# A hybrid decoder trunk: linear attention's scores as five products, mixers' operands in halves of 64 columns, and attention's second value product over half the keys

## The chip, the core and the metric

The kernel runs on one core of one Trainium2 chip. Its engines work side by side, each through its own instructions in order: TensorE (PE; PEld is its loading of weights), VectorE (DVE), ScalarE (ACT), GpSimd (POOL) and SyncE (SP, which here only starts DMAs). PE writes to PSUM banks; DVE and ACT copy from there to SBUF. The metric is the device time of one execution in microseconds, lower is better.

## What is computed

Two layers, 1024 tokens, model width 1024, everything in f32. A layer projects the normalised input once, feeds three groups of heads (the "mixers"), gates their outputs and projects back. The three mixers, cut to what the change touches:

```python
def sliding_window_attention(q, k, v, sinks):          # 8 heads of 64, 2 kv heads, blocks of 128
    kk, vv = with_prev(kb), with_prev(vb)              # a block sees its own keys and the block before
    rel = i + ATTN_BLOCK - j
    valid = (rel >= 0) & (rel < WINDOW)                # 128 keys back, the own one included
    p = softmax(concatenate([where(valid, s, -1e30), sink]))[..., :-1]
    return einsum('bnhgqk,bnkhd->bnqhgd', p, vv)

def retention(q, k, v):                                # 4 heads of 64, chunks of 128
    def step(state, inp):
        sc = einsum('bhid,bhjd->bhij', qi, ki) * dmask
        intra = einsum('bhij,bhjv->bhiv', sc, vi)
        inter = einsum('bhid,bhdv->bhiv', qi * q_decay, state)
        return chunk_decay * state + einsum('bhjd,bhjv->bhdv', ki * k_decay, vi), intra + inter

def gated_linear_attention(q, k, v, log_a):            # 4 heads, key width 32, value width 64
    def step(state, inp):
        b = cumsum(gi, axis=2)                         # per key channel
        decay = where(causal, exp(minimum(b_i - b_j, 0.0)), 0.0)
        sc = einsum('bhid,bhijd,bhjd->bhij', qi, decay, ki)
        intra = einsum('bhij,bhjv->bhiv', sc, vi)
        inter = einsum('bhid,bhdv->bhiv', qi * exp(b), state)
        return exp(b_last) * state + einsum('bhjd,bhjv->bhdv', ki * exp(b_last - b), vi), intra + inter
```

## The kernel before

Tokens are tiled by 128: eight tiles t, four pairs p. A layer runs through the columns of the projection in units of 256 (`do_gqk`, `do_kv` and so on). The projections are products of f32r halves into the three PSUM banks called `mm`; all the rest on PE, the mixers' products and the transposes, goes to the five banks called `aux`, which are handed out in turn. Each mixer is a generator, a "job": `attn_two` (two tiles of one kv head g), `ret_two` (two tiles of retention), `gla_decays` and `gla_core` (two chunks of linear attention).

PE's order is written out while the program is recorded. A clock `clk` counts the cost that each product is said to have (`mult` adds it); a job that yields `lat(key, l)` is taken up again when `clk` has gone on by the number that the table `L` has under that key (with `@1` for the second layer), and meanwhile the projections are recorded. PE then runs what is recorded in that order and waits where an operand is late. The order on ACT, DVE, POOL and SP within a layer's body is the framework's scheduler's.

A product names an operand that is loaded as weights (`lhsT`, up to 128 rows and 128 columns) and one that streams past (`rhs`). Where operands start at other partitions than 0, or the weights have 64 or 32 columns, only a part of the array is used: a tile of so many rows and columns. In the profile "32*128" is such a shape of weights, rows by columns; a product of f32 operands shows up as two records (two passes), one of f32r as one.

The steps that the change touches, by the names that the profile has for them:

- linear attention's scores, in `gla_core`: for a chunk c and a head h (32 rows) three products of blocks (`kxz` by `q1`, 32 columns streaming) and four of the sub-blocks of 8 (`kds` by `ad`), 28 products for the four heads, each with 128 columns of weights ("aux<-t,mx" and "aux<-t" 32*128). Each head has its own `aux` bank, sp[h]. ACT (L1774) and DVE (L1775, under the mask `mask2`) copy them to `scz`.
- linear attention's value products: `qb` by the state `stG`, then `scz` by v ("aux<-t,mx" 128*128 128x64); then `pst`, the new state, in tiles of 32 columns ("aux<-t,t" 128*32).
- retention: scores of 64 rows by 128 columns ("aux<-t" 64*128), then the state product ("aux<-stR,t"), the values ("aux<-t,t" 128*128 128x64) and the new state `pst` ("aux<-t,t" 128*128 128x128).
- attention's value products in `attn_two`: the transposed softmax `pf` by the value tile of the block before ("aux<-t,va" 128*64), then the part of it that lies in the own block (`pr`, cut out on POOL at L1545) by the difference of the two value tiles, `vd` (made on POOL at L1497; "aux<-t,vd").
- the columns of the modulation in `mod_third` ("aux<-c_ones,acc").

Of the kernel before, what the change touches and what calls it, by code (L numbers as in the profile page):

```python
# [61 lines left out]
def host_constants():  # L62
# [9 lines left out]
    c["mask2"] = ((i[:, None] <= i[None, :]) & (i[:, None] // 32 == i[None, :] // 32)).astype(np.int32)  # L72
# [96 lines left out]
def trunk(ctx: ExitStack, tc: tile.TileContext, ins, cst, out):  # L169
# [242 lines left out]
    def mod_third(l, j):  # L412
# [17 lines left out]
        for hh in range(2):  # L430
# [1056 lines left out]
    def attn_two(l, ts, g, q):  # L1487

        sms, parts, pss = {}, {}, {}
        for t in ts:  # L1490
            sm = sms[t] = gp.tile([P, 4, 129], F32, tag="smx", name=nm("smx"), bufs=SMB)
            V.tensor_copy(sm[:, :, 128], sink8[:, l, 4 * g:4 * g + 4])
            if t == 0:
                G.memset(sm[:, :, 0:128], -1e30)
            else:
                vd = gp.tile([P, P], F32, tag="vd", name=nm("vd"), bufs=4)
                G.tensor_tensor(vd, kv["v"][t], kv["v"][t - 1], ALU.subtract)  # L1497
                parts[t] = vd
# [37 lines left out]
        for t in ts:  # L1536
# [5 lines left out]
            mv[t] = [(kv["v"][max(t - 1, 0)], pf)]  # L1542
            if t > 0:
                pr = t2()
                G.affine_select(h4(pr), h4(pf), [[0, 4], [1, P]], ALU.is_ge, 0.0, base=0, channel_multiplier=-1)  # L1545
                mv[t].append((parts[t], pr))
        yield lat("aq4", l)
        po = aux()
# [6 lines left out]
        copy("aoc", ao, po)  # L1555
# [117 lines left out]

    def cb32(ap):
        return ap.rearrange("p (c b i) -> p c b i", c=2, i=32)

    def gla_decays(l, p):
# [21 lines left out]
        midv = mid.rearrange("p (b s) -> p b s", s=4)  # L1699
        for s, dst in enumerate((dC[:, 0:64], dC[:, 64:192], dC[:, 192:384], dB[:, 256:512])):  # L1700
            n = 8 * s + 8
            eng(f"ak{s}").tensor_tensor(dst.rearrange("p (b i) -> p b i", i=n),
                                        midv[:, :, s:s + 1].to_broadcast((P, 8, n)), b32(bc)[:, :, 0:n], ALU.subtract)
# [15 lines left out]
    QSC = 32.0 ** -0.5  # L1719

    def gla_core(l, p, qk, vs):
# [7 lines left out]
        k = qk[:, 256:512]  # L1729
# [5 lines left out]
        for s, src in enumerate((dC[:, 0:64], dC[:, 64:192], dC[:, 192:384])):  # L1735
            n = 8 * s + 8
            eng(f"kd{s}").tensor_tensor(b32(kdz[:, s])[:, :, 0:n], b32(k)[:, :, 0:n],
                                        src.rearrange("p (b i) -> p b i", i=n), ALU.mult)
        kds = [kdz[:, 0], kdz[:, 1], kdz[:, 2], ad[:, 256:512]]
        for s in range(4, 0, -1):  # L1740
            kv_ = kxz[:, s - 1].rearrange("p c (b i) -> p c b i", i=32)
            eng(f"kx{s}").tensor_tensor(kv_[:, :, 0:s, :], cb32(k1)[:, :, 0:s, :],
                                        g[:, :, 4 * s:5 * s].unsqueeze(3).to_broadcast((P, 2, s, 32)), ALU.mult)
# [9 lines left out]
        for c in range(2):  # L1753
# [9 lines left out]
            yield lat("gcs", l)  # L1763
            for s in range(4):
                for h in range(4):
                    r = slice(32 * h, 32 * h + 32)
                    dst = sp[h][:, 0:P].rearrange("p (b i) -> p b i", i=32)[:, :, 8 * s:8 * s + 8]
# [705 lines left out]
```

## Time and profile before

| | us |
|---|---|
| median of 3 timed executions | 964.28 (964.02 to 966.57) |
| the profiled execution | 965.28 |
| its span, first to last instruction | 963.6 |
| PE busy in the span | 944.9 |
| DVE, ACT, POOL busy | 670.1, 392.7, 176.8 |
| mean granted clock of TensorE | 0.999 of full |

The profiled execution took 1.0 us more than the median of the others. The mixers' products on PE run from 108 to 430 us in the first layer and from 584 to 861 us in the second, between the projections' products; what lies ahead of and between the two prepares a layer or ends it, and the last output follows.

### The profile page before, as it was taken

How to read it: one execution, taken by the hardware profiler on the slowest of the kernel's cores; microseconds unless marked ns; L12 is line 12 of the kernel's file. 1: busy time of each engine (PE TensorE's matmuls, PEld its weight loads, DVE VectorE, ACT ScalarE, POOL GpSimd, SP SyncE). 2: the span in 40 equal slices, each digit the busy share in tenths (PEclk: the TensorE clock that was granted, in tenths of full speed). 3: DMA queues.
4: the chain of work that ended last, by engine and by line, in shares of the span. 5: the costliest groups of instructions: out<-in, count | busy, mean ns of one | idle time of the engine just before them, and what ended most of it. 6: DMA issues, size and time to landing. Idle time of an engine off the chain costs nothing.

```text
span 963.6 us, 19029 instructions
## 1 busy us (share of the span) xinstructions
PE 944.9 (98%) x7001; PEld 816.6 (85%) x7001; DVE 670.1 (70%) x1645; ACT 392.7 (41%) x1077; POOL 176.8 (18%) x227
## 2 busy tenths in 40 slices
PE   7999999999999999999999999999999999999996
PEld 5678999889988878778899998998899787778885
DVE  5899757557776878647486487774575487663896
ACT  4467212223314746534364232132332277641441
POOL 1020001122211223320120000101222034440301
PEclk9999999999999999999999999999999999999999
DMA  8944404433344456776555573461223333378883
GB/s 313 334 143 128 125 21 125 162 103 98 109 127 140 122 177 189 245 250 204 185 189 183 189 225 110 120 188 55 88 67 110 99 100 92 107 216 259 302 300 135
DMA packets 129677, 155.02 MB, mean 161 GB/s; under 512 B 13696, under 2 KB 93484, under 8 KB 128816
## 3 DMA queue, kind: packets, MB, share of 16 engines
q1 hardware_dynamic: 124752, 145.82, 47.9%
q10 hardware_dynamic: 4832, 7.99, 2.2%
q8 instruction: 55, 0.90, 0.4%
q14 instruction: 38, 0.31, 0.1%
HBM read 111.30 MB, written 40.37 MB: 157 GB/s over the span
## 4 chain that ended last, share of the span: by engine, by line
PE 71%; DMA 12%; DVE 8%; issue 4%; ACT 2%; SPq 1%; POOL 0%; ACTq 0%; DVEq 0%; POOLq 0%
PE mm L251 52%; PE aux L251 15%; PE aux L266 4%; DMA t<-aoS 2%; DMA su<-in_w_out_dram 2%; SPq L237 1%; DMA ma<-mixS 1%; DMA st<-in_w_mod_dram 1%; DMA wm<-in_w_mod_first_dram 1%; DMA st<-in_w_in_first_dram 1%; DMA st<-twS 1%; DMA st<-in_w_in_dram 1%; DVE arena L614 1%; DMA aoS<-t 1%; DMA c_freq<-cst_freq_dram 0%
## 5 line engine op out<-in xcount | busy, mean ns | idle before, releaser
L251 PE MATMUL mm<-arena,arena 128*128 128x256 f32 (+2 forms) x2808 | 467.2, 320 | 2.3 <-DVE arena L966 1.5
L251 PEld LDWEIGHTS mm<-arena,arena 128*128 128x128 f32 x2808 | 393.7, 188 | 45.4 <-issue 4.1
L251 PE MATMUL mm<-arena,mx 128*128 128x512 f32 (+1 forms) x564 | 128.1, 383 | 0.1
L251 PEld LDWEIGHTS mm<-arena,mx 128*128 128x128 f32 x564 | 101.7, 188 | 20.9 <-DMA mx<-mixS 1.0
L251 PE MATMUL mm<-arena 128*128 128x512 f32 (+2 forms) x624 | 110.9, 330 | 0.0
L251 PEld LDWEIGHTS mm<-arena 128*128 128x128 f32 x624 | 92.0, 188 | 11.4 <-issue 1.6
L762 POOL TENSOR_TENSOR sm<-sm,mhalf 128x1 f32<-128x1 f32 (+1 forms) x40 | 44.5, 1113 | 277.9 <-DVE sm L761 274.2
L232 ACT ACTIVATE arena<-st 128x512 fp32r<-128x512 f32 x91 | 54.3, 625 | 68.9 <-PE mm L251 29.5
L232 ACT ACTIVATE t<-aux 128x512 f32<-128x512 f32 (+1 forms) x86 | 47.8, 588 | 56.3 <-PE aux L266 26.5
L614 DVE TENSOR_TENSOR arena<-st,arena 128x512 fp32r<-128x512 f32 x96 | 67.1, 725 | 4.0 <-ACT arena L232 2.5
L1527 ACT ACTIVATE smx<-smx,sm 128x129 f32<-128x129 f32 x128 | 49.9, 393 | 17.0 <-DVE sm L1524 16.5
L448 DVE SCALAR_TENSOR_TENSOR acc<-st,c_act,acc 128x512 f32<-128x512 f32 x60 | 45.7, 761 | 15.4 <-DMA st<-in_w_mod_dram 12.9
L1531 POOL TENSOR_TENSOR smx<-smx,sm 128x512 f32<-128x512 f32 x32 | 34.3, 1072 | 77.8 <-DVE sm L1530 67.1
L251 PEld LDWEIGHTS aux<-t,mx 32*128 32x128 f32 (+1 forms) x896 | 41.1, 186 | 7.3 <-issue 3.9
L251 PE MATMUL aux<-t,mx 32*128 32x32 f32 (+1 forms) x896 | 43.8, 274 | 0.0
L266 PE MATMUL aux<-c_ident,t 128*128 128x128 f32 (+1 forms) x244 | 37.4, 276 | 0.9 <-DVE t L966 0.5
L232 ACT ACTIVATE t<-mm 128x256 f32<-128x256 f32 x40 | 14.8, 379 | 50.6 <-PE mm L251 46.7
L266 PEld LDWEIGHTS aux<-c_ident,t 128*128 128x128 f32 (+1 forms) x244 | 28.5, 140 | 5.8 <-DVE t L966 0.8
L1520 DVE COPY_PREDICATED smx<-c_curmask,aux 128x256 f32<-128x256 int32 x64 | 25.2, 447 | 8.5 <-ACT smx L232 7.8
L251 PE MATMUL aux<-t,t 128*128 128x64 f32 (+2 forms) x296 | 29.5, 256 | 1.6 <-DVE t L1839 1.6
L1775 DVE COPY_PREDICATED mx<-c_mask,aux 128x128 f32<-128x128 int32 x64 | 14.4, 298 | 21.6 <-ACT mx L1774 21.5
L251 PEld LDWEIGHTS aux<-kT,mx 64*128 64x128 f32 x384 | 24.0, 186 | 5.8 <-issue 3.1
(246 smaller groups left out, 1336.9 us busy)
## 6 DMA issues: line engine op xcount, KB each, us to landing
st<-in_w_in_dram SPq DMA_DIRECT2D x88, 256.0 KB
st<-in_w_mod_dram SPq DMA_DIRECT2D x64, 256.0 KB
mixS<-t SPq DMA_DIRECT2D x48, 256.0 KB
mx<-mixS SPq DMA_DIRECT2D x20, 512.0 KB
st<-in_w_out_dram SPq DMA_DIRECT2D x28, 256.0 KB
wm<-in_w_mod_first_dram SPq DMA_DIRECT2D x6, 1024.0 KB
t<-tabS SPq DMA_DIRECT2D x16, 256.0 KB
aoS<-t SPq DMA_DIRECT2D x32, 128.0 KB
```

The lines of the kernel that those rows point to most:

```text
L232: A.activation(dst, src, AF.Copy)
L237: i = {"S": nc.sync, "A": A, "P": G}[EN[k]].dma_start(dst, src)
L251: T.matmul(dst, lhsT, rhs, start=start, stop=stop)
L266: T.transpose(dst, src, idn)
L448: V.scalar_tensor_tensor(acc, wt, c_act[:, k:k + 1], acc, ALU.mult, ALU.add)
L614: e.tensor_tensor(lo, st, f(hi), ALU.subtract)
L762: G.tensor_tensor(r, r, mhalf[:, :w], ALU.pow)
L1520: V.copy_predicated(sv, curmask.unsqueeze(1).to_broadcast((P, 2, P)), pv[:, :, n // P - 1, :])
L1527: A.activation(sm[:, h, :], sm[:, h, :], AF.Exp, bias=mx[:, h:h + 1], accum_out=sums[:, h:h + 1])
L1531: eng("pn").tensor_tensor(sm[:, :, 0:128], sm[:, :, 0:128], rs.unsqueeze(2).to_broadcast((P, 4, P)), ALU.mult)
L1775: V.copy_predicated(scz[:, c, h, :], mask2, sp[h][:, 0:P])
```

## The change

**Linear attention's scores.** Each chunk of 128 is cut another way: five products in place of seven, and all weights but those of the first are taken in two halves of 64 columns (u), so that a product i consists of 4 heads by 2 halves, in tiles of 32 rows by 64 columns. Product 0: the second 64 queries by the first 64 keys. Product 1: the second block of 32 in each half by the first one. Product 2: the second 16 of each block of 32 by the first 16. Products 3 and 4: the two halves of 8 within blocks of 16. The decays that they need (`gla_decays`) are formed to match, and the scores come out of PSUM in four copies per head in place of two.

**Halves of 64 columns.** Linear attention's value products, all products of retention and the columns of the modulation take their weights in two halves of 64 columns, each into 64 output partitions. Retention's new state forms only the four 64x64 blocks that it keeps.

**Attention's values.** The value tile v[t] now holds the first 64 keys of block t and the last 64 of block t-1. Half the queries u of a block streams at a time; the first product takes all 128 keys of v[t], the second only the 64 keys (rows o of `parts[t]`) that this half of the queries has otherwise. `vd` is made in two halves, `pr` is half as wide, and the result lies in two `aux` banks in place of one. A ninth `va` buffer is added.

The table `L` has other waits in 31 places, most by less than 1.5 (`gc2` 6.25 to 4.41, `mod6` 13.38 to 9.7); `EN` names the engines of the new copies ("gcx" ACT, "vd0", "vd1", "kx0" POOL). The recorded cost per product is set so that a chunk's scores sum to the same 1.51 as before (28 by 0.054, 36 by 0.042).

```diff
+    near = (i[:, None] <= i[None, :]) & (i[:, None] // 16 == i[None, :] // 16)
+    half = (i[:, None] // 32 == np.arange(4)[None, :]) & (i[:, None] % 32 < 16)
+    c["mask2"] = np.concatenate([near, half], axis=1).astype(np.int32)
...
-                    mult(pm[:, b:b + 1], acc[:, b * P:(b + 1) * P], ones[:, 0:1], True, True)
+                    for u in range(2):
+                        o = slice(64 * u, 64 * u + 64)
+                        mult(pm[o, b:b + 1], acc[:, b * P:(b + 1) * P][:, o], ones[:, 0:1], True, True, 0.105)
...
-        v[t] = gp.tile([P, P], F32, tag="va", name=nm("va"), bufs=VDB)
-        A.activation(v[t], pk[:, 128:256], AF.Copy)
+        for i in range(t + 1 if t else 0, t + 2):
+            v[i] = gp.tile([P, P], F32, tag="va", name=nm("va"), bufs=VDB)
+        A.activation(v[t][0:64], pk[0:64, 128:256], AF.Copy)
+        for i in range(t + 1 if t else 0, t + 2):
+            A.activation(v[i][64:P], pk[64:P, 128:256], AF.Copy)
...
-                G.tensor_tensor(vd, kv["v"][t], kv["v"][t - 1], ALU.subtract)
+                eng("vd0").tensor_tensor(vd[0:64], kv["v"][t - 1][0:64], kv["v"][t][0:64], ALU.subtract)
+                eng("vd1").tensor_tensor(vd[64:P], kv["v"][t + 1][64:P], kv["v"][t][64:P], ALU.subtract)
...
         for i, t in enumerate(ts):
-            for q_, (vt, pvv) in enumerate(mv[t]):
+            for u in range(2):
                 for r in range(2):
-                    mult(po[64 * r:64 * r + 64, 256 * i:256 * i + 256].rearrange("p (j n) -> p j n", j=2),
-                         vt[:, 64 * r:64 * r + 64], h4(pvv)[:, r:4:2, :], q_ == 0, q_ == len(mv[t]) - 1, 0.215)
+                    mult(into(u, i, r), kv["v"][t][:, 64 * r:64 * r + 64], h4(mv[t][0])[:, r:4:2, 64 * u:64 * u + 64],
+                         i == 0, False, 0.11)
+        for i, t in enumerate(ts):
+            for u in range(2 if t else 0):
+                o = slice(64 * u, 64 * u + 64)
+                for r in range(2):
+                    mult(into(u, i, r), parts[t][o, 64 * r:64 * r + 64], mv[t][1][o, r:4:2], False, i == 1, 0.055)
...
-            for s in range(1, 4):
-                for h in range(4):
-                    r = slice(32 * h, 32 * h + 32)
-                    mult(sp[h][:, P + 32 * s:P + 32 * s + 32], kxz[r, s - 1, c],
-                         q1[r, P * c + 32 * s:P * c + 32 * s + 32], True, True, 0.054)
...
-                    mult(dst, kds[s][r, P * c:P * c + P], cb32(ad[:, 0:256])[r, c, :, 8 * s:8 * s + 8],
-                         True, True, 0.054)
+            for i in range(5):
+                for h in range(4):
+                    for u in range(2 if i else 1):
+                        r, o = slice(32 * h, 32 * h + 32), slice(64 * u, 64 * u + 64)
+                        d = sp[h][o]
+                        if i == 0:
+                            mult(d[:, 192:256], kxz[r, 0, c, o], kxz[r, 2, c, 64:128], True, True, TILE)
+                        elif i == 1:
+                            mult(d[:, 160 + 96 * u:192 + 96 * u], kxz[r, 1, c, o], cb32(q1)[r, c, 1 + 2 * u], True, True,
+                                 TILE)
+                        elif i == 2:
+                            mult(d[:, 288:352], kdz[r, 1, cs][:, o], kdz[r, 2, 64 * c:64 * c + 64], True, True, TILE)
+                        else:
+                            e = slice(8 * (i - 3), 8 * (i - 3) + 8)
+                            mult(b16(d[:, 0:P])[:, :, e], (kdz[:, 0], ad[:, 256:512])[i - 3][r, cs][:, o], q8[r, :, e],
+                                 True, True, TILE)
...
-                A.activation(scz[:, c, h, 32:P], sp[h][:, P + 32:2 * P], AF.Copy)
-                V.copy_predicated(scz[:, c, h, :], mask2, sp[h][:, 0:P])
+                d, z_ = sp[h], scz[:, c, h]
+                A.activation(z_[0:64, 32:P], d[0:64, 160:256], AF.Copy)
+                V.copy_predicated(z_, mask2[:, 0:P], d[:, 0:P])
+                copy("gcx", z_[64:96, 96:P], d[64:96, 256:288])
+                V.copy_predicated(b32(z_)[:, :, 16:32], mask2[:, P:P + 4].unsqueeze(2).to_broadcast((P, 4, 16)),
+                                  b16(d[:, 288:352]))
...
-                mult(po[:, 64 * h:64 * h + 64], scz[:, c, h], v[:, 64 * h:64 * h + 64],
-                     t == 0, t == 0 or h == 3)
+                for u in range(2):
+                    o = slice(64 * u, 64 * u + 64)
+                    mult(po[o, 64 * h:64 * h + 64], scz[:, c, h, o], v[:, 64 * h:64 * h + 64],
+                         t == 0, t == 0 or h == 3, 0.105)
...
-                for j in range(2):
-                    mult(pst[:, j * P:(j + 1) * P], k[:, j * P:(j + 1) * P], v[:, j * P:(j + 1) * P], True, True)
+                for h in range(4):
+                    e = slice(64 * h, 64 * h + 64)
+                    mult(pst[64 * (h % 2):64 * (h % 2) + 64, 64 * (h // 2):64 * (h // 2) + 64], k[:, e], v[:, e], True,
+                         True, 0.06)
```

Where instructions stand now, at three places. The first is PE at the scores of the first pair of chunks in the first layer: `aux_2477` and the three after it are the banks of the four heads of chunk 0, `aux_2541` that of head 0 of chunk 1, `mm_...` projections, `mx_2130` the tile that holds `kxz` and `kdz`. Before, heads 0 and 1 of the first product, head 0 of the fourth and of the last, and what follows:

```order
L266 MATMUL aux_2472<-c_ident,mx_2130 128x128 x2
L251 MATMUL aux_2477<-t_390_2365,mx_2130 128x32
L251 MATMUL aux_2478<-t_390_2365,mx_2130 128x32
...
L251 MATMUL aux_2477<-t_391_2366,mx_2130 128x4x8
...
L251 MATMUL aux_2477<-t_391_2366 128x4x8
...
L251 MATMUL mm_2460<-arena_143,arena_73 128x256 x17
L251 MATMUL mm_2536<-arena_513,arena_73 128x512 x4
L251 MATMUL aux_2541<-t_390_2365,mx_2130 128x32
```

With the change, head 0 of each of the five products and the last one of all, and what follows (`aux_2547` and on are the banks now, `aux_2625` that of the next chunk):

```order
L268 MATMUL aux_2542<-c_ident,mx_2189 128x128 x2
L253 MATMUL aux_2547<-mx_2189 64x64
...
L253 MATMUL aux_2547<-t_390_2457,mx_2189 64x32 x2
...
L253 MATMUL aux_2547<-mx_2189 64x64 x2
...
L253 MATMUL aux_2547<-t_391_2458,mx_2189 64x8x8 x2
...
L253 MATMUL aux_2550<-t_391_2458 64x8x8 x2
L253 MATMUL mm_2508<-arena_143,arena_73 128x256 x3
L253 MATMUL mm_2612<-arena_143,arena_73 128x256 x7
L253 MATMUL aux_2620<-acc_1890,c_ones 128x512
L253 MATMUL aux_2625<-mx_2189 64x64
```

Seven rows per head have become one and four pairs. Between the scores of chunk 0 and those of chunk 1 stand 10 projection products and one of the modulation, where 17 and 4 longer ones stood.

The second is DVE at the same place, copying chunk 0's scores out of the four banks. Before, and then with the change:

```order
L1775 COPY_PREDICATED mx_2132<-c_mask_145,aux_2477 128x128
L1775 COPY_PREDICATED mx_2132<-c_mask_145,aux_2478 128x128
L1775 COPY_PREDICATED mx_2132<-c_mask_145,aux_2479 128x128
L1775 COPY_PREDICATED mx_2132<-c_mask_145,aux_2480 128x128
...
L1775 COPY_PREDICATED mx_2132<-c_mask_145,aux_2541 128x128
```

```order
L1815 COPY_PREDICATED mx_2191<-c_mask_145,aux_2547 128x128
L1815 COPY_PREDICATED mx_2191<-c_mask_145,aux_2548 128x128
L1815 COPY_PREDICATED mx_2191<-c_mask_145,aux_2549 128x128
L1817 COPY_PREDICATED mx_2191<-c_mask_145,aux_2547 128x4x16
L1815 COPY_PREDICATED mx_2191<-c_mask_145,aux_2550 128x128
L1817 COPY_PREDICATED mx_2191<-c_mask_145,aux_2548 128x4x16
L1817 COPY_PREDICATED mx_2191<-c_mask_145,aux_2549 128x4x16
L1817 COPY_PREDICATED mx_2191<-c_mask_145,aux_2550 128x4x16
```

Each head has a second copy, which follows ACT's copy of a 32x32 block; the first three heads' first copies go ahead of all second ones, so the heads overlap.

The third is PE at retention's values and new state for tile 1 of the first layer (`aux_1452` and `aux_1465` are the output, `stR` the state). Before, and then with the change:

```order
L251 MATMUL mm_1493<-arena_143,arena_73 128x256 x14
L251 MATMUL aux_1452<-stR,t_224_1319 128x128
L251 MATMUL aux_1452<-t_211_1241,t_230_1346 128x64 x2
...
L251 MATMUL aux_1514<-t_211_1241,t_204_1176 128x128 x2
L251 MATMUL mm_1493<-arena_143,arena_73 128x256 x10
```

```order
L253 MATMUL mm_1526<-arena_73,arena_513 128x272 x7
L253 MATMUL aux_1465<-stR,t_224_1326 64x128 x2
L253 MATMUL aux_1465<-t_211_1241,t_234_1376 64x64 x4
...
L253 MATMUL aux_1546<-t_211_1241,t_204_1176 64x64 x4
L268 MATMUL aux_1554<-c_ident,t_250_1505 128x128 x4
```

Every product stands there in two halves, and the group stands between products of the full width as before.

More of the change, by code (lines that the diff above doesn't have):

```diff
@@ L1698, in gla_decays @@
                         mid.unsqueeze(2).to_broadcast((P, 32, 8)), ALU.subtract)
[L1699 to L1703, printed above, removed]
+        half = b32(bw)[:, :, 15:16].to_broadcast((P, 8, 16))
+        eng("ak0").tensor_tensor(dC[:, 0:128].rearrange("p (m i) -> p m i", i=8),
+                                 mid[:, 0::2].unsqueeze(2).to_broadcast((P, 16, 8)), b16(bc)[:, :, 0:8], ALU.subtract)
+        eng("ak1").tensor_tensor(b16(dC[:, 128:256]), b32(bw)[:, :, 16:32], half, ALU.subtract)
+        eng("ak2").tensor_tensor(b16(dC[:, 256:384]), half, b32(bw)[:, :, 0:16], ALU.subtract)
+        eng("ak3").tensor_tensor(b16(dB[:, 256:512]), mid[:, 1::2].unsqueeze(2).to_broadcast((P, 16, 16)), b16(bc),
+                                 ALU.subtract)
         yield lat("gdb", l)
@@ L1734, in gla_core, with grown @@
         yield lat("gca", l)
[L1735 to L1743, printed above, removed]
+        eng("kd0").tensor_tensor(b16(kdz[:, 0])[:, :, 0:8], b16(k)[:, :, 0:8],
+                                 dC[:, 0:128].rearrange("p (m i) -> p m i", i=8), ALU.mult)
+        eng("kd1").tensor_tensor(b32(kdz[:, 1])[:, :, 0:16], b32(k)[:, :, 0:16], b16(dC[:, 256:384]), ALU.mult)
+        eng("kd2").tensor_tensor(b16(kdz[:, 2, 0:128]), b32(q)[:, :, 16:32], b16(dC[:, 128:256]), ALU.mult)
+        def grown(i, at, src, by):
+            d = kxz[:, i].rearrange("p c (b i) -> p c b i", i=32)[:, :, at]
+            n = d.shape[2]
+            eng(f"kx{i}").tensor_tensor(d, cb32(src)[:, :, at], by.unsqueeze(3).to_broadcast((P, 2, n, 32)), ALU.mult)
+        grown(3, slice(0, 4), k1, g[:, :, 16:20])
+        grown(2, slice(2, 4), q1, g[:, :, 3:14:10])
+        grown(0, slice(0, 2), k1, g[:, :, 8:10])
+        copy("kx1", kxz[:, 1].rearrange("p c (b i) -> p c b i", i=32)[:, :, 0:4:2], cb32(k1)[:, :, 0:4:2])
         yield lat("gcb", l)
@@ L1832, in ret_two @@
                 c = (h // 2) * P
-                mult(sp[h % 2][:, 256 * i + c:256 * i + c + P], tts[t][r, 256 + c:256 + c + P], tts[t][r, c:c + P],
-                     True, True)
+                for u in range(2):
+                    o = slice(64 * u, 64 * u + 64)
+                    mult(sp[h % 2][o, 256 * i + c:256 * i + c + P], tts[t][r, 256 + c:256 + c + P][:, o],
+                         tts[t][r, c:c + P], True, True, 0.105)
         scs = {}
@@ L1850, in ret_two @@
             for j in range(2):
-                if t > 0:
-                    mult(po[:, j * P:(j + 1) * P], qT[:, j * P:(j + 1) * P], stR[:, j, :], True, False)
+                for u in range(2 if t > 0 else 0):
+                    o = slice(64 * u, 64 * u + 64)
+                    mult(po[o, j * P:(j + 1) * P], qT[:, j * P:(j + 1) * P][:, o], stR[:, j, :], True, False, 0.11)
                 for h in (2 * j, 2 * j + 1):
-                    mult(po[:, 64 * h:64 * h + 64], sc[:, h * P:(h + 1) * P], v[:, 64 * h:64 * h + 64],
-                         t == 0, t == 0 or h % 2 == 1)
+                    for u in range(2):
+                        o = slice(64 * u, 64 * u + 64)
+                        mult(po[o, 64 * h:64 * h + 64], sc[:, h * P:(h + 1) * P][:, o], v[:, 64 * h:64 * h + 64],
+                             t == 0, t == 0 or h % 2 == 1, 0.105)
             if t < NT - 1:
                 pst = aux()
-                for j in range(2):
-                    mult(pst[:, j * P:(j + 1) * P], k[:, j * P:(j + 1) * P], v[:, j * P:(j + 1) * P], True, True)
+                for h in range(4):
+                    e = slice(64 * h, 64 * h + 64)
+                    mult(pst[64 * (h % 2):64 * (h % 2) + 64, 64 * (h // 2):64 * (h // 2) + 64], k[:, e], v[:, e], True,
+                         True, 0.06)
                 for c in range(2):
```

43 lines of the change are left out of this document (26 added, 17 removed).

## The prediction

> **What bounds the kernel now.** I read the page's shares first, then the windows of the two stretches in which the mixers run, then what PE waited for.
>
> ```profile
> PE 944.9 (98%) x7001; PEld 816.6 (85%) x7001; DVE 670.1 (70%) x1645; ACT 392.7 (41%) x1077; POOL 176.8 (18%) x227
> PE 71%; DMA 12%; DVE 8%; issue 4%; ACT 2%; SPq 1%; POOL 0%; ACTq 0%; DVEq 0%; POOLq 0%
> ```
>
> ```profile
> core 0: us, PE busy (x) PEld busy (x) DVE busy (x) ACT busy (x) POOL busy (x), PEclk, DMA share, GB/s
> 187.00:300.00 113.00, 113.00 (x1185) 103.23 (x1185) 76.88 (x225) 33.50 (x102) 22.51 (x38) 1.00 0.38 114
> 300.00:400.00 100.00, 100.00 (x641) 79.92 (x638) 80.67 (x157) 61.36 (x195) 30.94 (x38) 1.00 0.53 159
> 690.00:770.00 80.00, 80.00 (x829) 71.18 (x828) 49.96 (x159) 23.61 (x73) 18.04 (x24) 1.00 0.27 88
> 770.00:845.00 75.00, 74.69 (x524) 57.57 (x523) 55.64 (x116) 55.02 (x197) 32.17 (x39) 1.00 0.35 103
> ```
>
> In all four windows PE is busy from end to end, at the full clock, while DVE has 19 to 38% to spare and the DMA engines about half or more. "Busy" says little for an engine whose records overlap, so the waits matter more: PE's longest inside these stretches is
>
> ```profile
> engine line waited for: us in total, times, longest us
> PE aux L251 <- POOL t L1545: 0.6, 1, 0.6
> ```
>
> So the time of the mixers' stretches is the time that PE's records take one after another. What is saved there shortens the run, until something else comes late.
>
> **What a record costs.** The durations in a row of PE overlap; the cost is the distance from one group's start to the next one's. Four groups show it:
>
> ```profile
> 158.51 7.57 PE L251 MATMUL mm<-arena,arena 128*128 128x256 f32 x62
> 165.92 0.38 PE L251 MATMUL aux<-stR,t 128*128 128x128 f32 x2
> 166.14 0.56 PE L251 MATMUL aux<-t,t 128*128 128x64 f32 x4
> 166.53 0.44 PE L251 MATMUL aux<-stR,t 128*128 128x128 f32 x2
> 166.81 1.06 PE L251 MATMUL aux<-t,t 128*128 128x64 f32 x8
> 167.70 0.60 PE L266 MATMUL aux<-c_ident,t 128*128 128x128 f32 x4
> ...
> 205.79 1.54 PE L251 MATMUL aux<-t,mx 32*128 32x32 f32 x48
> 207.15 0.40 PE L251 MATMUL aux<-t 32*128 32x32 f32 x8
> 207.48 3.20 PE L251 MATMUL mm<-arena,arena 128*128 128x256 f32 x21
> ...
> 328.75 1.08 PE L251 MATMUL aux<-t,va 128*64 128x256 f32 x8
> 329.67 0.60 PE L251 MATMUL aux<-t,vd 128*64 128x256 f32 x4
> 330.20 2.11 PE L251 MATMUL mm<-arena,arena 128*128 128x512 f32 x8
> ```
>
> Projections with 256 columns streaming: 62 records in 7.41 us, 0.12 each. Retention's values: 16 records in 1.78 us, 0.111 each, whether 128 or 64 columns stream. Linear attention's scores: 56 records in 1.69 us; in fours (the heads lie in different rows) that is 14 passes, and 14 x 0.111 = 1.56 leaves 0.13 for the change of shape. Attention's values: 12 records in 1.45 us; in pairs (two column halves) six passes of 0.215, and 0.16 left. What sets the 0.111 is the weights:
>
> ```profile
> L251 PEld LDWEIGHTS aux<-t,mx 128*128 128x128 f32 x128 | 16.8, 191 | 0.9
> L251 PEld LDWEIGHTS aux<-t,vd 128*64 128x64 f32 x112 | 7.9, 137 | 5.2 <-POOL t L1545 1.4
> L251 PEld LDWEIGHTS aux<-t,t 128*32 128x32 f32 x112 | 2.2, 108 | 0.9
> ```
>
> The mean load of 64 columns is 0.054 us shorter than that of 128, that of 32 another 0.029 shorter; so a load costs 0.83 ns a column, 0.106 for 128 and 0.053 for 64, beside a fixed part that overlaps. Streaming costs the same per column: 0.215 for 256, so 0.107 for 128 and 0.054 for 64. A pass takes the longer of the two and some 0.003 to 0.005 more. Halves of 64 columns therefore pay where 64 columns stream (0.111 becomes **0.057** for both halves, if these run side by side, as attention's do), and nothing where 128 stream (0.108). Next, a change of shape:
>
> ```profile
> 221.60 1.00 PE L251 MATMUL aux<-t,mx 128*128 128x64 f32 x8
> 222.53 0.32 PE L251 MATMUL aux<-t,t 128*32 128x64 f32 x8
> 222.78 0.23 PE L266 MATMUL aux<-c_ident,t 16*128 16x16 f32 x1
> ```
>
> The second group is two passes of 0.054, but 0.25 long: 0.03 is its first load, which nothing covers, and 0.11 a gap. I take 0.10 of gap and the first load: **0.15** into a shape of 64 columns, **0.20** back to 128.
>
> **The sum**, chunk by chunk (16 chunks, eight tiles in two layers):
>
> 1. Linear attention's scores. Before 1.56. Now five products of two passes, the first in four tiles, the others in eight. By load and stream a pass costs 0.057, ten make 0.57: the lower end. But it now issues 16 instructions, and the closest that PE's instructions are seen is
>
> ```profile
> 222.53 0.16 PEld L251 LDWEIGHTS aux<-t,t 128*32 128x32 f32 x8
> ```
>
> eight loads in 0.16, of which the last takes 0.108, so 7 ns apart. At 16 x 0.0067 = 0.107, eight passes cost 0.86 and the two of product 0 0.11 more: 0.97. The other end is the fastest long stream of this trace, the scores themselves: 112 instructions in 1.56, 14 ns each; 144 at that rate take 2.0. I take 0.97, the row of the nearest shape: 0.59 saved, 16 x 0.59 = **9.4**; the ends are +16 and -7. The first load is shorter by 0.05 where PE enters: once a chunk in the first layer, three times in the second (where the job pauses twice between products, by `gcs@1`), 32 x 0.05 = **1.6**.
> 2. Linear attention's values: eight passes from 0.111 to 0.057 save 0.43; the state product (256 columns stream) nothing; going in costs 0.15, and the way out leads to the new state as before. 0.28 x 14; the last chunk has no new state and pays 0.20 out: 0.08 x 2. **4.1**.
> 3. Retention's values and state: 16 x 0.111 = 1.78 becomes 4 x 0.108 + 8 x 0.057 + 4 x 0.057 = 1.11, and 0.35 in and out, since the group stood in the full shape: 0.32 x 12. The first tile lacks the four state passes (0.30 x 2), the last the new state (0.09 x 2). **4.6**.
> 4. Retention's scores stream 128 columns: only the first load, 0.05 x 8 = **0.4**.
> 5. Attention's values, a pair of tiles: 8 x 0.215 = 1.72 becomes 8 x 0.108, 0.15 into tiles of half the rows, 4 x 0.108: 1.45; 0.27 x 12. In the first pair tile 0 has no second product: 1.29 becomes 1.23, 0.06 x 4. **3.5**.
> 6. The modulation's columns: 0.43 saved, 0.35 spent, four times: **0.3**.
>
> Together 23.9 us. Against this stands what comes late. The scores' copies now are four a head: DVE has 64 more, ACT 64 more, and neither shape is in the trace. The two that there were, and a narrow one of ACT:
>
> ```profile
> L1774 ACT ACTIVATE mx<-aux 128x96 f32<-128x96 f32 x64 | 10.8, 255 | 28.6 <-PE aux L251 28.6
> L1775 DVE COPY_PREDICATED mx<-c_mask,aux 128x128 f32<-128x128 int32 x64 | 14.4, 298 | 21.6 <-ACT mx L1774 21.5
> L1620 ACT ACTIVATE ga<-mm 128x32 fp32r<-128x32 f32 x8 | 1.5, 191 | 0.9 <-PE mm L251 0.5 <-PE aux L266 0.4
> ```
>
> 0.3 and 0.19 at most, some 19 and 12 us of two engines that have that time; at least nothing. They cost something only by the banks that they hold:
>
> ```profile
> 144.92 1.02 PE L251 MATMUL aux<-acc,c_ones 128*128 128x512 f32 x2
> 145.37 2.56 PE L251 MATMUL mm<-arena,arena 128*128 128x256 f32 x17
> ...
> 207.57 0.68 ACT L1774 ACTIVATE mx<-aux 128x96 f32<-128x96 f32 x4 [1.29 <-PE aux L251]
> 207.96 0.89 DVE L1775 COPY_PREDICATED mx<-c_mask,aux 128x128 f32<-128x128 int32 x4
> 210.61 1.43 PEld L251 LDWEIGHTS aux<-t,mx 32*128 32x128 f32 x48 [0.36 <-ACT t L232]
> ```
>
> The last bank came free at 208.85, 1.37 after PE had left the scores at 207.48, and PE came back at 210.61. Four more copies on DVE, 0.2 apart as these are, make 2.2; a last handoff to ACT and back makes it 2.6. In the order of the change PE comes back after 1.9 (10 projection products of 0.12, one of the modulation of 0.45, 0.2 of switching) in the first pair, 2.3 in the next two, 2.5 or more in the other five: a wait of 0.3 to 0.7, three times, so 1.5. The halved `vd` and `pr` on POOL, the copies of v on ACT and attention's second bank each hold a buffer a little longer or shorter than before; the second product now follows both tiles' first ones, so it asks for POOL's `pr` no sooner. For waits of this kind that I can't place I set 2.5: PE is ahead of its recorded clock by what it saves, and jobs were timed against that clock. Bounds: 0, and half the gain. 23.9 - 4.0 = **19.9**. From the profiled execution's 965.28 that leaves 945.4; it took 1.0 more than the median of the timed ones, so the forecast is 944.4, said as 944.
>
> **The rivals.**
>
> *PE can't issue so densely.* Each record of the scores would cost what it costs now, 1.56 / 56 = 28 ns, however many tiles there are: 72 records, 2.0 us, a loss of 0.44 a chunk where I have a gain of 0.59. 16 x 1.03 = 16.5 less: 961. For it: no long stream in the trace is faster. Against: in that stream the loads alone explain the pace, and single bursts go at 7 ns. The Trainium skill speaks for it: "TensorE: Matmul & The Clock Gate", section "Wait — 56ns, not 53.3ns?", has the starts of matmuls never closer than about 25 ns, however few columns stream; by that my estimate for the scores is 72 x 0.025 = 1.8 and the run's time 958. The burst at 222.53 disagrees for different tiles, but it has only eight records.
>
> *Waits eat half.* DMAs hold 12% of the chain of waits already, and DVE is 81% busy in the window from 300 us. If PE comes to wait for half of what it saves, 12 in place of 4: 952.
>
> *Stream-bound scores.* The lower end of step 1 holds: 6.4 more saved, 938, and 936 without the waits I set.
>
> *Slower.* The four copies of a head write overlapping columns of `scz`, so each waits for the one before, across ACT and DVE. If the heads run one after another, 0.255 + 0.298 + 0.19 + 0.298 is 1.04 a head and 4.2 a chunk, 2.0 beyond the 2.2 or so that PE is away: 16 x 2.0 = 32 us of waits, 965.3 - 23.9 + 32 - 1.0 = 972. It decides from 1.5 a chunk (23.9 / 16). Against it: the order has three first copies ahead of any second one.
>
> *It does nothing.* If the column halves ran one after another, step 2 would lose its switch (0.17 a chunk in place of the gain, 7 us worse in all) and step 3 would pay its products with 128 columns streaming twice (0.8 lost a chunk, 17 us worse): 968. Attention's pairs of records, 0.215 for two halves of 64 columns, speak against it.
>
> **How the numbers follow.** Forecast, 939 to 950: 0.58. Stream-bound, 935 to 939: 0.09. Half eaten, 950 to 957: 0.15. No denser issue, 957 to 963: 0.10. It does nothing, 963 to 968: 0.04. Slower, 968 and more: 0.04. The range from 935 to 957 holds the first three, 0.82. 0.3% of the time, 2.9 us, is about what a measurement of this kernel can tell from no change. Faster by more: 0.58 + 0.09 + 0.15 and half of the next, 0.87; within it 0.08; slower 0.05.
>
> **What would show it.** Step 1: the records of the scores of a chunk in the first layer take about 1.1 us from their first start to the projection behind them, with the switch, in place of 1.69; 0.7 or 2.1 would be the ends. Steps 2 and 3: rows of 64 columns with 64 streaming come in pairs 0.057 apart, and a group of retention takes 1.5 in place of 1.78, most of a fifth of it switching. Step 5: 1.45 + 0.16 for a pair. The waits: rows of PE behind L1815, L1817 or POOL of more than 4 us in all would say that the cover was thinner than I read it. The forecast is wrong if PE's waits grow by more than 10 us, or if a pass of eight tiles takes more than 0.16 us.

## The result, and the profile after

| | before | after |
|---|---|---|
| median, us | 964.71 (964.02 to 966.57, 4 runs) | 947.94 (946.61 to 950.46, 4 runs) |
| ratio, with its 95% interval | | 0.9826 (0.9801 to 0.9852) |
| profiled execution, us | 965.28 | 948.50 |
| its span | 963.6 | 946.7 |

The change takes 16.8 us off; the forecast was 944, its range 935 to 957. One execution of a later run (the one without pauses, 1013.9 us at a mean granted clock of 0.849) is left out of its median. The page after, busy times and the shares of the chain of waits:

```profile
PE 922.0 (97%) x8053; PEld 788.5 (83%) x8053; DVE 686.0 (72%) x1709; ACT 409.0 (43%) x1175; POOL 203.6 (22%) x283
PE 60%; DVE 15%; DMA 14%; issue 5%; ACT 3%; POOL 2%; SPq 1%; ACTq 0%; DVEq 0%; POOLq 0%
```

PE is busy 22.9 us less, and DVE holds 15% of the chain in place of 8: span less PE's busy time grew from 18.7 to 24.7. The records show where the 22.9 come from. A chunk's scores in the first layer, first and last row and the projection behind (start, length, operation, count):

```profile
202.29 0.28 PE L253 MATMUL aux<-mx 32*64 32x64 f32 x4
...
202.95 0.39 PE L253 MATMUL aux<-t 32*64 32x64 f32 x12
203.27 1.40 PE L253 MATMUL mm<-arena,arena 128*128 128x256 f32 x10
```

From 202.29 to 203.27 are 0.98 us, where 205.79 to 207.48 were 1.69. Linear attention's values, and retention's with the projection ahead (of before, then after):

```profile
236.79 0.65 PE L253 MATMUL aux<-stG,t 128*64 128x256 f32 x4
237.27 0.64 PE L253 MATMUL aux<-t,mx 128*64 128x64 f32 x16
237.83 0.32 PE L253 MATMUL aux<-t,t 128*32 128x64 f32 x8
238.08 4.13 PE L253 MATMUL mm<-arena,arena 128*128 128x256 f32 x34
```

```profile
186.28 0.99 PE L251 MATMUL mm<-arena,arena 128*128 128x256 f32 x7
187.11 0.38 PE L251 MATMUL aux<-stR,t 128*128 128x128 f32 x2
...
188.81 1.90 PE L251 MATMUL mm<-arena,arena 128*128 128x256 f32 x14
```

```profile
185.20 0.99 PE L253 MATMUL mm<-arena,arena 128*128 128x256 f32 x7
186.12 0.44 PE L253 MATMUL aux<-stR,t 128*64 128x128 f32 x4
...
187.41 2.28 PE L253 MATMUL mm<-arena,arena 128*128 128x256 f32 x17
```

Retention's group takes 1.29 in place of 1.70. The price of the change of shape stands one row higher: the same seven projection products last 0.92 up to the group, 0.83 before, so 0.09 for going in. Linear attention's group takes 1.30 (1.61 before), also with 0.09 ahead. Attention's pair, undisturbed, and then where it stands worst:

```profile
407.32 1.09 PE L253 MATMUL aux<-t,va 128*64 128x128 f32 x16
408.35 0.67 PE L253 MATMUL aux<-t,vd 64*64 64x128 f32 x16
408.95 2.33 PE L253 MATMUL mm<-arena,mx 128*128 128x512 f32 x9
```

```profile
389.68 1.09 PE L253 MATMUL aux<-t,va 128*64 128x128 f32 x16
391.70 0.45 PE L253 MATMUL aux<-t,vd 64*64 64x128 f32 x8 [0.93 <-POOL t L1555]
393.32 0.45 PE L253 MATMUL aux<-t,vd 64*64 64x128 f32 x8 [1.17 <-POOL t L1555]
393.70 1.70 PE L253 MATMUL aux<-kT,mx 64*128 64x256 f32 x24
```

1.63 in place of 1.88 (a pair of before: 427.14 to 429.01); but with the two waits 4.02. They are for `pr`, and POOL's own rows tell why. First the timeline (with what ended the idle time ahead), of after and of before, then the groups (busy us, mean ns), of after and of before:

```profile
389.11 1.04 POOL L1539 TENSOR_TENSOR smx<-smx,sm 128x512 f32<-128x512 f32 x1 [5.65 <-DVE sm L1538]
390.11 0.60 POOL L1554 TENSOR_SCALAR_AFFINE_SELECT t<-t 128x256 f32<-128x256 f32 x1
390.78 0.87 POOL L1555 TENSOR_SCALAR_AFFINE_SELECT t<-t 64x256 f32<-64x256 f32 x1
391.61 0.85 POOL L1554 TENSOR_SCALAR_AFFINE_SELECT t<-t 128x256 f32<-128x256 f32 x1
392.52 0.74 POOL L1555 TENSOR_SCALAR_AFFINE_SELECT t<-t 64x256 f32<-64x256 f32 x1
```

```profile
393.01 1.04 POOL L1531 TENSOR_TENSOR smx<-smx,sm 128x512 f32<-128x512 f32 x1 [4.49 <-DVE sm L1530]
394.00 1.22 POOL L1545 TENSOR_SCALAR_AFFINE_SELECT t<-t 128x512 f32<-128x512 f32 x2
```

```profile
L1554 POOL TENSOR_SCALAR_AFFINE_SELECT t<-t 128x256 f32<-128x256 f32 x28 | 15.2, 542 | 8.5 <-DMA mixS<-t 4.8 <-ACT t L234 2.1 <-DMA t<-t 1.6
L1555 POOL TENSOR_SCALAR_AFFINE_SELECT t<-t 64x256 f32<-64x256 f32 x28 | 14.9, 533 | 1.9
```

```profile
L1545 POOL TENSOR_SCALAR_AFFINE_SELECT t<-t 128x512 f32<-128x512 f32 x28 | 21.5, 784 | 5.0 <-DMA t<-t 3.6 <-ACT t L232 1.1 <-DMA mixS<-t 0.2
```

POOL cuts three quarters as many elements as before, in two instructions of 0.54 where one of 0.78 was. It starts only behind the softmax of another unit (L1539), which waits for DVE; that was so before too (L1531), but the two selects that followed took 1.22 there (up to 2.2 at other pairs), and the four that follow here now take 3.1. PE's longer waits after, from 100 us on:

```profile
PE aux L253 <- POOL t L1555: 2.5, 3, 1.2
PE aux L253 <- ACT t L234: 1.0, 2, 0.7
PE aux L268 <- DVE mx L1817: 0.9, 2, 0.7
PE aux L268 <- DVE t L805: 0.9, 1, 0.9
PE aux L268 <- ACT t L1785: 0.8, 1, 0.8
```

Counted by the starts of all products, group by group, with 0.09 for each new way in, PE's records are 25.3 us shorter: scores 12.7, linear attention's values 3.3, retention 5.0 and its scores 0.4, attention 3.3, modulation 0.6. From its first product to its last PE needs 16.8 less, so waits took about 8.5: 2.7 around the scores, 3.0 more than before inside attention's values, the rest in pieces up to 1.0. (Busy time has 22.9 and 6.0 for the two: a product's end is modelled, and hides part of a wait.) The two layers differ: after 1800 of the 4160 records into the `mm` banks, behind the first layer's mixers, PE is 4.7 us ahead of before (441.85, now 437.15), after 3840, behind the second's, 16.5 (866.6, now 850.1). Nearly the same is saved in each, some 12 and 13; the first layer's waits eat 7 of it, the second's 1.

### The profile page after: what moved, and what is told of

Its sections match the earlier page's. It is cut to its first block, busy times and chain, and to the rows that moved or that the text cites. A ratio compares the mean times of both kernels' runs of the same rounds, so it can differ in the third digit from the quotient of the medians.

```text
span 946.7 us, 21353 instructions
## 1 busy us (share of the span) xinstructions
PE 922.0 (97%) x8053; PEld 788.5 (83%) x8053; DVE 686.0 (72%) x1709; ACT 409.0 (43%) x1175; POOL 203.6 (22%) x283
## 4 chain that ended last, share of the span: by engine, by line
PE 60%; DVE 15%; DMA 14%; issue 5%; ACT 3%; POOL 2%; SPq 1%; ACTq 0%; DVEq 0%; POOLq 0%
PE mm L253 45%; PE aux L253 11%; PE aux L268 4%; DMA t<-aoS 2%; DMA su<-in_w_out_dram 2%; DVE arena L618 1%; DMA st<-in_w_out_dram 1%; SPq L239 1%; DMA aoS<-t 1%; POOL sm L766 1%; DMA mixS<-t 1%; DMA st<-in_w_in_dram 1%; DMA wm<-in_w_mod_first_dram 1%; ACT smx L1535 1%; DMA st<-twS 1%
## 5 line engine op out<-in xcount | busy, mean ns | idle before, releaser
L234 ACT ACTIVATE t<-aux 128x512 f32<-128x512 f32 (+2 forms) x102 | 49.1, 521 | 48.2 <-PE aux L268 23.9
L1539 POOL TENSOR_TENSOR smx<-smx,sm 128x512 f32<-128x512 f32 x32 | 34.5, 1078 | 71.4 <-DVE sm L1538 67.6
L2381 DVE SCALAR_TENSOR_TENSOR t<-t,t 128x512 f32<-128x512 f32 x16 | 11.9, 741 | 27.0 <-DMA t<-aoS 25.4
L253 PE MATMUL aux<-kT,mx 64*128 64x256 f32 (+1 forms) x384 | 27.3, 287 | 0.2 <-ACT t L234 0.2
L1969 DVE SCALAR_TENSOR_TENSOR t<-t,sm,t 128x512 f32<-128x512 f32 x16 | 11.5, 752 | 21.8 <-DMA t<-in_x_dram 20.3
L234 ACT ACTIVATE smx<-aux 128x256 f32<-128x256 f32 x56 | 18.3, 385 | 20.9 <-PE aux L253 20.4
```

The source lines that it names most:

```text
L234: A.activation(dst, src, AF.Copy)
L253: T.matmul(dst, lhsT, rhs, start=start, stop=stop)
L1539: eng("pn").tensor_tensor(sm[:, :, 0:128], sm[:, :, 0:128], rs.unsqueeze(2).to_broadcast((P, 4, P)), ALU.mult)
L1969: V.scalar_tensor_tensor(xt[j], yg[j], r, xt[j], ALU.mult, ALU.add)
L2381: V.scalar_tensor_tensor(ao, th, 0.5, ao, ALU.mult, ALU.mult)
```

## Experiments: what the table of waits is worth

The first four take the change apart. Scores alone, on the kernel before with before's table; then the change without them:

```diff
-            for s in range(1, 4):
...
+            for i in range(5):
+                for h in range(4):
+                    for u in range(2 if i else 1):
...
```

> The kernel before with the scores' five products alone (their decays, operands, mask and four copies a head), and before's table of waits. Theory, records: in the trace after the change a chunk's scores take 0.98 us on PE in the first layer where they took 1.69, and 0.36 + 0.42 + 0.30 = 1.08 in the second where they took 0.80 + 0.58 + 0.58 = 1.96; 8 x 0.71 + 8 x 0.88 = 12.7 us, of which PE gives back 2 to 3 by waiting for the four banks: 10 us under before, 953 to 956 against 964.7. Rival, waits eat half: 958 to 960. Rival, the re-timed table is what lets it in: with the old table less than 3 us of gain, 962 or more.

> The changed kernel with before's seven products for the scores and all the rest as changed, the table too. Theory, records: 12.7 us of PE come back and the 2 to 3 us of waits for score banks go, so 10 us over the changed kernel's 947.9: 956.5 to 959.5. If the parts don't add up (PE's other savings are only worth something together with the scores), it is near before, 963 or more; if the table brings the gain, 951 or less.

958.04 (955.1 to 960.3; ratio to before 0.9918, 0.9893 to 0.9943) and 957.72 (957.3 to 960.1; 0.992, 0.9899 to 0.9941). The second falls where the records put it. The first has gained with the old table, so that rival is out, but 2 us less than its range wanted, at the lower edge of "waits eat half": the scores are worth 7.8 us on before (965.8 in these runs) and 9.8 within the changed kernel. Attention's values as before:

```diff
...
-                    mult(into(u, i, r), parts[t][o, 64 * r:64 * r + 64], mv[t][1][o, r:4:2], False, i == 1, 0.055)
...
+                         vt[:, 64 * r:64 * r + 64], h4(pvv)[:, r:4:2, :], q_ == 0, q_ == len(mv[t]) - 1, 0.215)
...
```

> The changed kernel with before's value products in attention, and with them its value tiles, vd, pr, one result bank and eight va buffers. Theory, records and POOL: PE's records take 0.26 more for each of 12 pairs and 0.05 for 4, 3.3 us, while the waits inside these groups (3.96 us in the changed kernel's trace, 0.95 in before's) lose 3.0: within 1.5 us of the changed kernel, 946.5 to 949.5. Rival, my prediction's term as it stood: 951 to 952. Rival, POOL's and ACT's added work costs elsewhere too: 946 or less.

949.28 (947.5 to 949.9; 0.9824, 0.9802 to 0.9846): no difference to the changed kernel. The 3.3 us of records are there, but in this run's trace the waits inside attention's values are 1.6 us, in the changed kernel's 4.0, most of both behind POOL's select: 2.4 of the 3.3 go back there, and the rest is within the scatter. The prediction's term of 3.5 did not arrive. Then the table (three of its 31 entries):

```diff
-"gc2": 4.41, "mod6": 9.7, "rc1": 4.91
+"gc2": 6.25, "mod6": 13.38, "rc1": 4.48
...
```

> The changed kernel with before's table of waits. Theory, records: PE's groups take the same as with the new table, only waits move; gc2 (6.25 in place of 4.41) and mod6 (13.38 in place of 9.7) are the largest moves and lie off the path, so 948 to 952, PE's waits up by 0 to 4. Rival, the table brings most of the gain: 957 or more. Rival, the table is no better than the old one: 946 to 948.

963.21 (959.0 to 966.5; 0.997, 0.9951 to 0.9989). This I had not expected: with the 31 old numbers 15 of the 17 us are gone, though PE's groups take what they take with the new ones. Its longest waits, but for the start (the changed kernel's were shown above):

```profile
PE aux L253 <- ACT t L234: 3.9, 2, 2.8
PE aux L253 <- DVE t L1888: 3.6, 2, 2.1
PE aux L253 <- DVE smx L1528: 2.9, 3, 1.3
```

Span less PE's busy time is 34.3 (24.7 with the new table). Another 3 us went at one place and appear in no wait. Windows of 1 us; after the engines' busy times and counts stand the granted clock, the DMA share and GB/s:

```profile
237.00:238.00 1.00, 0.09 (x1) 0.00 (x1) 1.00 (x6) 0.56 (x3) 0.00 (x0) 1.00 0.03 8
...
240.00:241.00 1.00, 0.00 (x0) 0.00 (x0) 1.00 (x3) 0.23 (x2) 1.00 (x2) 0.66 0.00 0
241.00:242.00 1.00, 0.89 (x5) 0.92 (x6) 0.56 (x3) 0.38 (x3) 0.14 (x1) 0.50 0.25 35
...
246.00:247.00 1.00, 1.00 (x7) 1.00 (x6) 1.00 (x2) 0.38 (x1) 0.00 (x0) 0.50 1.01 333
247.00:248.00 1.00, 1.00 (x14) 0.72 (x14) 0.80 (x2) 0.00 (x0) 0.12 (x1) 0.93 0.72 133
```

PE stood in 237 to 238 and in 240 to 241; the clock was at half from 240.3 to 247.1, and PE worked for six microseconds of that. Is the new table simply better?

```diff
-"gc2": 6.25, "mod6": 13.38, "rc1": 4.48
+"gc2": 4.41, "mod6": 9.7, "rc1": 4.91
...
```

> The kernel before with the new table of waits and nothing else of the change. Theory, the table only fits the order to the shorter records: PE's records stay as they are, and with nothing saved there is nothing to fit, so 962 to 970. Rival, it is a better table whatever the records: 957 or less, since taking it away from the changed kernel cost 15 us.

965.12 (962.9 to 967.4; 0.9997, 0.998 to 1.0014): nothing. Is it its entries at the place where most was lost?

```diff
-"gc1": 0.71, "gc2": 6.25, "gc4": 0.61, "gd3": 15.53, "gdb": 1.49, "gdc": 0.4
+"gc1": 0.68, "gc2": 4.41, "gc4": 0.72, "gd3": 16.06, "gdb": 1.42, "gdc": 0.51
```

> The changed kernel with before's table, but six entries for linear attention in the first layer (gc1, gc2, gc4, gd3, gdb, gdc) new. With the old table the projections between 231 and 250 us fell 7.0 us behind: PE stood 2.9 us at the score banks and their operands, and 6.4 us then ran at half the clock. Theory, a table's entries act at their own places: most of these 7 us come back, 955 to 958. Rival, the waits only move on to the next late operand: 960 or more.

963.54 (960.1 to 967.3; 0.9972, 0.995 to 0.9993): the waits moved on, and the profiled execution has four spells of half clock (from 181.6, 239.6, 396.6 and 594.6 us), each behind a wait. Two more runs close the cube of scores, halves (with attention's values) and table; their edits are those above, combined.

> The changed kernel with before's seven score products and before's table: the halves of 64 columns and attention's value product alone. Together with e1, e2, e4 and e5 this leaves one corner open of the cube scores by halves by table. Theory, it is the amount: with either part alone PE gains about 12 us of records and the order still fits under both tables, only both parts together run ahead of the other engines: 956 to 960 (with the new table 957.7). Rival, the table was fitted to the halves: their jobs come too early without it, 963 or more. Rival, the table always brings something with the halves: 960 to 963.

> The kernel before with the five score products alone, as the first experiment, but with the new table: the other open corner. Theory, amount: the table does nothing for one part alone, 956 to 960 (with the old table 958.0). Rival, the table is fitted to the scores: 952 to 955, the full 12.7 us of records. Rival, the table fits only the whole change: 962 or more.

| median, us | old table | new table |
|---|---|---|
| neither part (in these runs 965.6 to 966.0) | 965.6 | 965.1 |
| scores | 958.0 | 958.6 |
| halves | 968.1 (960.6 to 972.2) | 957.7 |
| both | 963.2 | 947.9 |

The expectation "it is the amount" fell: the scores alone don't care for the table (0.9926, 0.9913 to 0.994 with the new one), the halves alone bring nothing without it (1.0019, 0.9996 to 1.0042) and 8 us with it. What differs? The score products report the same sum to the clock as before, the halves do not. So the last run takes before's table and gives them before's sums:

```diff
-                         True, 0.06)
+                         True, 0.32/3)
...
-                         i == 0, False, 0.11)
+                         i == 0, False, 0.43/3 if t else 0.1075)
...
-                        mult(pm[o, b:b + 1], acc[:, b * P:(b + 1) * P][:, o], ones[:, 0:1], True, True, 0.105)
+                        mult(pm[o, b:b + 1], acc[:, b * P:(b + 1) * P][:, o], ones[:, 0:1], True, True, 0.015)
...
```

> The changed kernel with before's table, and with the costs that the halves report to the clock set so that each group adds what it added before (the change has a retention tile's new state at 0.24 in place of 0.43, attention's values at 0.66 a tile in place of 0.86, the modulation's columns at 0.84 in place of 0.12; what PE executes in each group is unchanged). Then every job stands between the same projection products as in the kernel before; with the old table and the change's own costs 19 of the 110 groups of transposes and 13 of the 58 groups of retention's state products, linear attention's, attention's values and keys' products, stood elsewhere. Theory, the order: what cost 15 us is that the new costs moved jobs while the table that goes with them was missing, so the old order with the old costs keeps most of the records' 25 us: 947 to 953. Rival, the speed: PE runs ahead of the other engines in any order that was timed for the longer records: 958 to 965.

In its trace every group of the mixers' products and transposes stands behind as many projection products as in before's; with the old table and the change's own costs 19 groups of transposes, 4 of the two state products, 6 of attention's values, 3 of the keys' products and 2 of the scores stood elsewhere. 956.01 (952.1 to 958.7; 0.9899, 0.9878 to 0.992), between the two theories. The moved order is 7 of the 15 us (963.2 to 956.0). The other 8 (to 947.9) the new table, with the costs that go with it, brings even against before's order; both with about 3 either way. How they are made up stays open in part: the profiled run was the fastest of the six, 3.6 us over the changed kernel's; it has two spells of half clock, 1.7 us each, and 1.7 more of idle PE, so some 1.5 goes the other way.

## Experiments: the scores' width, and two attempts to do better

```diff
-                    for u in range(2 if i else 1):
-                        r, o = slice(32 * h, 32 * h + 32), slice(64 * u, 64 * u + 64)
+                    for u in range(1):
+                        r, o = slice(32 * h, 32 * h + 32), slice(64 * u, 64 * u + (128 if i else 64))
...
```

> The changed kernel with the five products' weights in one piece of 128 columns in place of two halves (product 1 streams both its blocks of 32, so half of what it and product 1's halves write is not used). Theory, loads: before, 14 passes of four tiles with 128 columns took 1.49 us without the way out, 0.106 each; eight such passes, 0.12 for product 0 and 0.20 out make 1.17 us where the halves take 0.98: 16 x 0.19 = 3.0 us slower, 950 to 952. Rival, the number of instructions sets the time (16.6 ns per product, 72 records against 40): 0.98 becomes 0.6, 5 us faster, 942 to 944. If the halves were worth as much as the change of the cut (the prediction's 0.111 against 0.057 a pass): 8 x 0.05 x 16 = 6.9 slower, 954 to 956.

956.63 (954.9 to 959.6; 0.9908, 0.9883 to 0.9934). The scores of a chunk, products 0, 1 and 4 and the projection behind:

```profile
204.52 0.34 PE L253 MATMUL aux<-mx 32*64 32x64 f32 x8
204.79 0.45 PE L253 MATMUL aux<-t,mx 32*128 32x64 f32 x8
...
205.51 0.40 PE L253 MATMUL aux<-t 32*128 32x64 f32 x8
205.84 0.84 PE L253 MATMUL mm<-arena,arena 128*128 128x256 f32 x5
```

1.32 us with 40 records, 0.98 with 72: the number of instructions doesn't set it, so the rival fell. Products 1 to 3 take 0.72 from 204.79 to 205.51, 0.12 a pass, near the 0.111 that a load of 128 columns sets. In the second layer a chunk takes 1.63 in place of 1.08; so of the scores' 12.7 us the halves are 7.1 (8 x 0.34 and 8 x 0.55) and the new cut 5.6. The time lies by the third expectation, not the first, 8.7 over the changed kernel, of which 7.1 are these records. The profiled execution, the slowest of the six, also has one spell of half clock (from 398.6 us).

```diff
-"gcs@1": 0.62
+"gcs@1": 0.0
```

> The changed kernel with gcs@1 at 0: a chunk's scores in the second layer are recorded in one piece, as in the first, in place of three. Theory, records: 1.08 us in three pieces becomes 0.98, and two more entries from a projection, 0.09 each, go: 0.28 x 8 = 2.2 us, 944.5 to 947 against 947.9. Rival, the pauses cover DVE's and POOL's making of the operands, or the shift of the order puts PE in front of something late: 948 to 953.

956.6 in five runs (953.6 to 961.2; 0.9911, 0.9879 to 0.9944), 9 slower in place of 2 faster. In the profiled execution (955.3, so 6.8 over) nearly all of it is lost in the second layer, where PE now stands for operands that come late. The longest waits of the run are these, 2.8 and 2.3 us of them in the second layer, and the clock was at half for 3.4 us behind one wait in the first layer (from 394.0) and two in the second (711.5 and 779.7), 1.7 us each:

```profile
PE aux L253 <- ACT t L234: 3.7, 4, 1.8
PE aux L268 <- ACT t L1785: 3.1, 3, 1.3
```

Last, the order of a head's copies, with PE's order untouched:

```diff
-                V.copy_predicated(z_, mask2[:, 0:P], d[:, 0:P])
                 copy("gcx", z_[64:96, 96:P], d[64:96, 256:288])
+                V.copy_predicated(z_, mask2[:, 0:P], d[:, 0:P])
```

> The changed kernel with ACT's copy of the 32x32 block (gcx) written ahead of DVE's first copy of a head, so that a head's chain changes engine once in place of three times. PE's order stays as it is, row for row. Theory, banks: PE's waits inside the groups of scores, 2.7 us in the changed kernel's trace (2 or 3 of them behind DVE's last copy), shrink by 1 to 2 and nothing else moves: 945.5 to 947.5. Rival, the banks come free when DVE is through with its own queue, whatever ACT does: 947.5 to 949. Rival, DVE's and ACT's moved order makes something else late: 950 or more.

950.48 (947.8 to 952.9; 0.9842, 0.9822 to 0.9862): no gain. Time inside the scores' groups is 19.5 us after 19.1, which fits the first rival, that the banks come free when DVE gets to them; whether it is slower the runs can't tell. Nothing that was run beats the change as it is.

## Why the prediction was right

- *Step 1, the scores*: forecast 9.4 + 1.6, measured 12.7. The term was right in kind and too small: it set 16 instructions to 0.107 us, 6.7 ns each. In the middle of a chunk a product (two loads, two records on PE) starts every 16.6 ns, 4.2 an instruction; a pass of eight tiles is 0.067, not 0.107, close to the stream's 0.057. The second layer, in three pieces, saves 0.88 a chunk (0.36 + 0.42 + 0.30 in place of 0.80 + 0.58 + 0.58), the first 0.71.
- *Step 2, linear attention's values*: 4.1, measured 3.3. The eight passes save 0.37, not 0.43, and the state's product costs 0.05 more in halves; the way in costs 0.09, not 0.15.
- *Step 3, retention*: 4.6, measured 5.0. That it came so close is luck in part: the group that the prediction read took 1.78, but nearly all others 1.70, and with the way in the group takes 1.38 now, not 1.46; the two errors cancel. Step 4: 0.4 and 0.4. Step 6: 0.3 and 0.6.
- *Step 5, attention's values*: 3.5, measured 3.3 of records and nothing in time. The step that failed is "the second product now follows both tiles' first ones, so it asks for POOL's `pr` no sooner": it asks no sooner, but `pr` is two selects a tile now, so it comes later (four took 3.1 us at 390 us, where before's two took 1.2 to 2.2).
- *The waits*: 4.0, measured 8.5. The 1.5 behind the banks in the first layer came (1.4, though not at the first pair), with 1.3 in the second that I had left out. The 2.5 for waits that I couldn't place was the weak number: it should have been 6. The sign that it named, over 4 us behind L1815, L1817 or POOL, stood at 3.4; the rest came behind others, in pieces. The reading of the waits before was a little off as well: the 0.6 behind POOL stands at 413.6 us, outside the four windows, and PE's longest wait among the mixers was 1.6 behind DVE's L1839 at 586 us. The sum doesn't use either.

The two errors, 1.4 too little saved and 4.5 too little lost, go against each other, and what is left of them is why 944 is 4 below the median (by the profiled executions 16.8 saved, 19.9 forecast). Of the rivals, denser issue being impossible fell with the records of the scores. By the Trainium skill ("TensorE: Matmul & The Clock Gate", section "Wait — 56ns, not 53.3ns?") starts are never closer than about 25 ns; here the starts of products in different tiles are 8 ns apart on average, so that floor doesn't hold across tiles. "Slower" asked for 32 us of waits around the scores, where 2.7 were found, and "it does nothing" fell with linear attention's groups (1.30 in place of 1.61). "Waits eat half" was nearer than the forecast made it: the table in the diff was counted as a detail, and it decides between 948 and 963.

## What to carry to other kernels

Where a recorded order meets other engines at given moments, a saving on the bounding engine can be worth little until the order is timed again: here 25 us of records brought under 3 us with the old waits and 17 with new ones, and one entry set to 0 cost 9. It isn't always so: the scores alone, which report the same cost as before, brought 7 to 8 of their 12.7 us with either table. So run a part alone with both tables before judging it, and keep reported costs equal where the order shall not move. Halving weights to 64 columns paid where the load set the pace, and each group paid 0.09 us to get in; count what the smaller operands cost the engine that makes them, since two smaller selects on POOL took 1.08 us for one of 0.78.

## What was not expected of the hardware

The clock. After short stands PE's granted clock was 0.50 for about 3.4 us, or twice that, which costs up to 1.7 us for each 3.4 and appears in no wait. It isn't a matter of the stand alone. The changed kernel at 391 us (columns as in the windows above) and the run with the copies moved have the same two waits, 0.93 or 0.94 and 1.17 us, at the same place:

```profile
392.00:393.00 1.00, 0.15 (x8) 0.00 (x0) 1.00 (x4) 0.00 (x0) 0.93 (x2) 1.00 1.02 395
393.00:394.00 1.00, 0.68 (x12) 0.51 (x14) 1.00 (x2) 0.15 (x1) 1.00 (x2) 1.00 0.98 336
394.00:395.00 1.00, 1.00 (x22) 1.00 (x20) 0.82 (x1) 0.81 (x4) 1.00 (x2) 1.00 0.68 163
```

```profile
391.00:392.00 1.00, 0.00 (x0) 0.00 (x0) 1.00 (x3) 0.00 (x0) 0.93 (x2) 1.00 0.94 287
392.00:393.00 1.00, 0.89 (x10) 0.56 (x12) 1.00 (x2) 0.11 (x1) 1.00 (x2) 0.57 0.78 258
394.00:395.00 1.00, 1.00 (x12) 1.00 (x12) 0.51 (x1) 0.58 (x2) 0.88 (x3) 0.50 1.02 372
```

The first keeps its clock, the second drops to 0.50 until about 395.5. A stand of 2.8 us (177.5 to 180.3 us with the old table) passed without a drop. The traces show what decides. In all 14 of them every change of the granted clock lies on a grid of 3.41 us, which lies elsewhere in each execution. Between 20 and 930 us 14 spells of half clock begin (none in the traces of before, of the change, of the scores alone or undone, of attention undone or of the table alone), and ahead of each PE was idle for 1.4 to 2.1 us of the window that ended there. All twelve windows with 1.6 or more idle were followed by a drop, two of the seven with 1.4 to 1.6, and none with less. The changed kernel's two waits fall into two windows, 0.93 and 1.17, the other run's into one, 2.11; the stand of 2.8 was cut into 1.31 and 1.48. So where the grid happens to lie decides whether a stand of this length costs 1.7 us more.

The Trainium skill ("TensorE: Matmul & The Clock Gate", section "Part 1: The HAM clock gate") has the clock halved after an idle window of some 3.4 us that runs freely; the length, the half and the chance agree with these traces, but no full idle window is needed: 1.4 us of a window were enough once, and 1.6 always. It would also fit that kernels in which PE stands more scatter more (959.0 to 966.5 with the old table, 946.6 to 950.5 with the new one). The mean granted clock of each execution bears that out in part: of the twelve of the halves alone with the old table, the two slowest (972.0 and 972.2 us) have two of the lowest clocks (0.990 and 0.987), the three fastest (960.6 to 962.8) the highest (0.996 and 0.997); the four of the changed kernel (0.994 to 0.996) show no such order.
